# A pair of query products written with seven block products, in a hybrid decoder layer

## The chip, the cores and the metric

The kernel runs on one core of a Trainium2 chip. The metric is the device time of one execution in microseconds (us). TensorE (PE) multiplies matrices, VectorE (DVE) and ScalarE (ACT) work elementwise, GpSimd (POOL) does a few elementwise operations and issues transfers, SyncE (SP) issues the loads of weights. Products accumulate in PSUM, which has eight banks of 128 x 512 numbers; everything else lies in SBUF or in device memory.

## The reference

One decoder layer over 256 tokens of width 2048, in float32: a feed-forward (width 5632), a mixer (windowed attention beside a recurrent part, both gated), a cross-attention into a memory of 256 tokens, a second feed-forward, a final norm. The part at hand is the first of the mixer:

```python
def gated_parallel_mixer(x, norm_g, w_in, sinks, ...):
    h = rms_norm(x, norm_g)
    p = h @ w_in
    c = np.cumsum([ATTN_WIDTH, KV_WIDTH, KV_WIDTH, RWKV_COLS]).tolist()
    q, k, v, p_rwkv, gates = jnp.split(p, c, axis=-1)
    y_attn = sliding_window_attention(q, k, v, sinks)
...
```

The queries `q` are the first 1024 columns of `p`: 16 heads of 64.

## The kernel before

**Numbers in two parts.** A float32 operand is held as a high part `hi` (rounded to the format that PE takes) and a low part `lo`, the rest. A product of two such operands is three matmuls: hi hi, hi lo, lo hi (`times`, L470 to L475; one line for each). Weights come from device memory into `raw` buffers; ACT casts `hi` from them (L396), DVE subtracts to get `lo` (L397). The normed activations are held in features x tokens, in `xhi` and `xlo`, 16 chunks of 128 features by 256 tokens; `Norm.block` (L681) makes four chunks from 512 columns of x by transposes on PE (L661), a cast on ACT (L688) and a subtraction on DVE (L689). The factor of the norm for each token, `r`, is applied to the product.

**A plain product** (`product`, L451) computes 256 tokens x 512 columns. It runs over the 16 chunks in eight pairs (`KU` = 2); for each pair it does two token blocks `t` x two chunks x three matmuls of 128 x 128 by 128 x 512. Its two sums stand in two banks of the `acc` ring (three banks).

**A product of pairs** (`product_pair`, L533) computes 256 tokens x two blocks of 512 columns at once. For a pair of chunks this is a product of a 2 x 2 by a 2 x 2 block matrix: eight block products, or seven by a scheme of Strassen's kind. For the seven it needs sums of the weights (`divide`, L425 to L428, four on DVE for a pair, then divided into `thi` and `tlo` by `two_parts`) and sums of the activations (`combinations`, L485: a sum of hi and lo, L505; four sums of 128 x 128 numbers, L511 to L514; a cast, L521; a subtraction, L524). The seven go to sums called p1 to p7 in PSUM: p1, p3, p5 in the `mm` ring, p2, p4 and q in `acc`, p6, p7 in `tr`, so all eight banks are in use. `first`, `middle` and `out` put them together. Which pairs of chunks are done with seven is a tuple in the plan of weights. The first feed-forward does gate and up so for three of eight pairs (`SEVEN`), its down products for three of eight or two of six.

**Order of the work.** `weight_plan` (L101) lists all weights in the order of use; from it come `units` (a block of 256 rows x 512 columns, 512 KB) and `items` (one unit, or two for a pair). `next_item` (L432) asks for the loads of the coming units, divides the weights of this item, and divides ahead up to `AHEAD` = 2 units. Loads go to SP's queue in that order. In the mixer the `raw` ring has four buffers of one unit; `hi` and `lo` rings have three of one unit each. In the feed-forwards loads use four buffers of two units (L341).

Background work (`Interleave`) is a set of generators that advance by a step at each `bg.tick()` between groups of matmuls. The compiler's planner then gives buffers out and orders each engine's instructions by estimated times, with the program's order as priority, so the order on an engine can differ from the program's a little. `tc.issue_after(ins)` puts an instruction behind another on its engine.

**At the change.** The last down product of the first feed-forward adds to x (L634), its columns are written out (L819) and turned into chunks 8 to 15 of the mixer's activations. Then the mixer begins: memory of the first stage is reused by its own pool, most of it a ring `t4` of 23 tiles of 4 KB a partition; a tile is reused when the one that lay there is free. The two plain products of L873 follow, each with eight items of one unit: `scaled` (L844) copies the two sums to `tok` with the factor `r` on ACT (L847), and `to_features` transposes them to `qt` (L866, L867) in the background. Then comes the product for keys and values (L879), and the attention (`attend`) behind it. `STAGE_AT` (L42) holds numbers of items at which sums of weights for the second feed-forward are made ahead.

Of the kernel before, what the change touches and what calls it, by code (L numbers as in the profile page):

```python
# [7 lines left out]
F32 = mybir.dt.float32  # L8
# [30 lines left out]
SEVEN, SEVEN_DOWN = (0, 2, 4), ((2, 4, 6), (2, 4))  # L39
SEVEN_2, STAGED = (0, 2, 3, 4), (3,)  # L40

STAGE_AT = [266 + 2 * n for n in range(10)]  # L42


class Act:
# [55 lines left out]
def weight_plan(a):  # L101

    w = {n: v[0] for n, v in a.items() if "_w_" in n or n.startswith("w_")}
    yield from feed_forward_plan(w["ffn1_w_gate"], w["ffn1_w_up"], w["ffn1_w_down"], False)
    yield None
    w_in = w["w_in"]
    cols = [0, 512, ATTN_W]
    for c in cols:  # L110
        yield w_in, 0, KD, c, 512
    yield w_in, 0, KD, C_RW + 3 * RW, 288
    for h in range(2):
        yield w_in, 0, KD, C_RW + RW + h * 512, 512
    for n in range(4):
        yield w_in, 0, KD, C_GATE + n * 512, 512
        yield w["w_proj_attn"], 0, 8, n * 512, 512
    for h in range(2):
        yield w_in, 0, KD, C_RW + h * 512, 512
        yield w_in, 0, KD, C_RW + 2 * RW + h * 512, 512  # L120
    for n in range(4):
        yield w_in, 0, KD, C_GATE + D + n * 512, 512
    for n in range(4):
        yield w["w_proj_rwkv"], 0, 8, n * 512, 512
    for n in range(4):
        yield w["w_out"], 0, KD, n * 512, 512
    yield w["w_cross_kv"], 0, KD, 0, 512
    yield w["w_cross_q"], 0, KD, 0, 512
    yield w["w_cross_kv"], 0, KD, 512, 512
    for n in range(4):  # L130
        yield w["w_cross_o"], 0, 4, n * 512, 512
    yield None
    yield from feed_forward_plan(w["ffn2_w_gate"], w["ffn2_w_up"], w["ffn2_w_down"], True)
# [3 lines left out]
def decoder_layer(ctx: ExitStack, tc: tile.TileContext, a: dict, out: bass.AP):  # L137
# [171 lines left out]
    for entry in weight_plan(a):  # L309
        if entry is None:  # L310
            ends.append(len(units))
            continue
        plan.append(entry)
        w, k0, nk, c0, n = entry
        if not isinstance(w, tuple):
            for k in range(k0, k0 + nk, KU):
                items.append(((len(units),), False))
                units.append((w, k, c0, n))
            continue
        for k in range(k0, k0 + nk, 2 * KU):  # L320
            u = len(units)
            units += [(v, k + i, c, 512) for v, c in zip(w, c0) for i in (0, KU)]
            for i in range(2):
                q = (k - k0) // KU + i
                if n == SEVEN_2 and q in STAGED:
                    staged[len(items)] = len(staged)
                items.append(((u + i, u + 2 + i), q in n))
    raws, parts, summed = {}, {}, {}
    first_unused = {items[i][0][1] for i in staged}
    sums_d = dram.tile([len(staged), P, 4, 512], F32, name="sums")  # L330
    at = {"item": 0, "product": 0, "pool": None}

    def load(u, pieces=None):

# [64 lines left out]

    def two_parts(v, e):  # L400
        sp = at["pool"]
        hi = sp.tile([P, KU, 512], F32R, tag="thi" + e, name="thi")
        lo = sp.tile([P, KU, 512], F32R, tag="tlo" + e, name="tlo")
        act.copy(hi[:], v[:])  # L404
        dve.tensor_tensor(lo[:], v[:], f32(hi[:]), ALU.subtract)  # L405
        return hi, lo

    def divide(i):


        if i >= len(items) or i in parts:
            return
        which, seven = items[i]
        if len(which) == 1:
            parts[i] = split_unit(*which)
            return
        g, u = which
        if not seven:
            parts[i] = split_unit(g), split_unit(u)
            return  # L420
        t = summed.get(i)
        if t is None:
            rg, ru = raws[g], raws[u]
            t = [wp.tile([P, KU, 512], F32, tag="raw", name="raw", bufs=4) for _ in range(2)]
            dve.tensor_tensor(t[1][:, 0], ru[:, 0], rg[:, 0], ALU.subtract)  # L425
            dve.tensor_tensor(t[0][:, 0], ru[:, 1], ru[:, 0], ALU.subtract)
            dve.tensor_tensor(t[0][:, 1], ru[:, 1], t[1][:, 0], ALU.subtract)  # L427
            dve.tensor_tensor(t[1][:, 1], rg[:, 1], t[0][:, 1], ALU.subtract)  # L428
        a_ = two_parts(t[0], "a")
        parts[i] = split_unit(g), split_unit(u, slice(1, 2)), (a_, two_parts(t[1], "b"))  # L430
# [54 lines left out]
    def combinations(sp, x: Act, seven, name, ready=lambda: True, early=True, n=0):  # L485

        pairs = [q for q in range(max(seven) + 1) if early or q in seven]
        n = n or sum(4 if q in seven else 2 for q in pairs)  # L490
        parts = [sp.tile([P, n, P], F32R, tag=name + e, name=name + e) for e in ("hi", "lo")]
        c = {"parts": parts, "at": {}, "done": False, "seven": seven, "early": early}

        def work():
            o = 0
            while not ready():
                yield
            for q in pairs:
                while not {2 * q, 2 * q + 1} <= x.done:
                    yield  # L500
                t = wp.tile([P, KU, 512], F32, tag="raw", name="raw", bufs=4)
                v = t[:, 0].rearrange("p (k t n) -> p k t n", k=2, t=2)
                f = t[:, 1].rearrange("p (i n) -> p i n", i=4)
                with tc.issue_after(at["lo"].ins):
                    dve.tensor_tensor(  # L505
                        t[:, 0].rearrange("p (k n) -> p k n", k=2), f32(x.at(0, 2 * q, 2)),
                        f32(x.at(1, 2 * q, 2)), ALU.add,
                    )
                if q in seven:
                    n = 4  # L510
                    dve.tensor_tensor(f[:, 0], v[:, 0, 1], v[:, 1, 1], ALU.add)  # L511
                    dve.tensor_tensor(f[:, 1], f[:, 0], v[:, 0, 0], ALU.subtract)
                    dve.tensor_tensor(f[:, 2], v[:, 0, 0], v[:, 0, 1], ALU.subtract)
                    dve.tensor_tensor(f[:, 3], v[:, 1, 0], f[:, 1], ALU.subtract)  # L514
                else:
                    n = 2
                    dve.tensor_tensor(f[:, :2], v[:, :, 0], v[:, :, 1], ALU.subtract)
                yield
                s = slice(o, o + n)
                with tc.issue_after(at["hi"].ins):  # L520
                    act.copy(parts[0][:, s], f[:, :n])  # L521
                yield
                with tc.issue_after(at["lo"].ins):
                    dve.tensor_tensor(parts[1][:, s], f[:, :n], f32(parts[0][:, s]), ALU.subtract)  # L524
                c["at"][q] = o
                o += n
                yield
            c["done"] = True

        bg.spawn("mem", work())  # L530
        return c

    def product_pair(x: Act, c, w, first, middle, out):  # L533
# [20 lines left out]
            return [x.at(p, k)[:, t * P : (t + 1) * P] for p in range(2)]  # L554

        def of_c(q, i):
            return [p[:, c["at"][q] + i, :] for p in c["parts"]]

        def of_w(parts_, i):
            return [p[:, i, :] for p in parts_]  # L560
# [1 line left out]
        for q in range(nk // KU):  # L562
            k = KU * q
            if q in seven:
                bg.until(lambda: c["done"] and (q > min(seven) or not bg.groups["feat"][1]))
                g, u, s = next_item()
                end = q == max(seven)
                ta, tb = s
                for i, (to, x_, w_) in enumerate((
                    ("p7", of_c(q, 2), of_w(ta, 0)), ("p6", of_c(q, 1), of_w(ta, 1)),  # L570
                    ("p1", of_x(0, k), of_w(g, 0)), ("p2", of_x(0, k + 1), of_w(g, 1)),
                    ("p3", of_c(q, 3), of_w(u, 1)), ("p4", of_x(1, k + 1), of_w(tb, 1)),
                    ("p5", of_c(q, 0), of_w(tb, 0)),
                )):
                    add(to, x_, w_, end and to in ("p1", "p5", "p6", "p7"))
                    if i % 2:
                        bg.tick()
                    if end and to == "p1":
                        first(b)
                if end:  # L580
                    middle(b)
                continue
            g, u = next_item()
            early, last = q < max(seven), q == nk // KU - 1
# [243 lines left out]
    with tc.tile_pool(name="mx", bufs=1, reuse_waits="tile") as sp:  # L828
# [3 lines left out]
        def t4(name, shape=(P, 4, T), dt=F32):  # L832
            return sp.tile(list(shape), dt, tag="t4", name=name, bufs=N4)

        for i, n in staged.items():
            bg.spawn("stage", stage(t4, i, n))

# [6 lines left out]
        def scaled(pb, r, n=512):  # L844
            s = t4("tok", (P, 2, 512))
            for t in range(2):
                act.activation(s[:, t, :n], pb[t][:, :n], AF.Copy, scale=r[t])  # L847
            return s

        C4 = [0, P, 2 * P, 3 * P]  # L850
# [14 lines left out]
        def to_features(tok, dst, name):  # L865
# [2 lines left out]
                yield  # L868
            bg.seen.add(name)

        qt = []
        for h in range(2):
            tok = scaled(product(n2.x, W["w_in"]), n2.r)  # L873
            qt.append(t4("qt"))
            bg.spawn("feat", to_features(tok, qt[h], "q"))

        kd = t4("kd")
        vt = t4("vt", (P, 2, KV_W))
# [760 lines left out]
```

## Time and profile before

| | |
|---|---|
| median of 3 runs | 2247.78 us (2247.43 to 2248.47) |
| profiled execution | 2248.79 us, of which the profile's span is 2247.1 us |
| PE busy | 2231.4 us (99%) |
| DVE busy | 1820.5 us (81%) |
| ACT busy | 1245.0 us (55%) |
| bytes moved | 461.35 MB, mean 205 GB/s |
| the two query products | from 715.3 us to about 762 us of the span |

A row of the timeline has the start and the duration in us, the engine, the line in the kernel, the operation, the tile written and the tiles read, shapes, a count, and in brackets the idle time before it with what ended it. A row of a stage has the stretch and its length, the busy time and count of instructions of PE, PEld (PE's loading of weights), DVE, ACT and POOL, the granted PE clock, the busy share of the transfer engines and GB/s. A row of grouped instructions has total busy us, mean ns of one, and the idle time of the engine just before them, with what ended it. Matmuls overlap one another, so a PE that is busy all the time can still go from one matmul to the next faster than a duration says: starts are what counts.

### The profile page before, as it was taken

The numbers are of one execution on the slowest core, as the hardware profiler recorded it, in microseconds if no ns is written. First come the engines' busy times: TensorE is split into PE (matmuls) and PEld (weight loads), VectorE is DVE, ScalarE is ACT, GpSimd is POOL, SyncE is SP. The second block draws the span as 40 slices with busy tenths as digits, with TensorE's granted clock in tenths as the row PEclk, the third lists the DMA queues.
The fourth block names the chain that finished last, engine by engine and source line by source line (L and its number), as shares of the span: only waits on it lengthen the run. The fifth ranks groups of instructions, "written<-read, shape, count | busy, mean of one in ns | idle before, by whom it ended". The sixth has DMA issues, their size and how long they took to land.

```text
span 2247.1 us, 28239 instructions
## 1 busy us (share of the span) xinstructions
PE 2231.4 (99%) x10587; PEld 1833.6 (82%) x10587; DVE 1820.5 (81%) x2342; ACT 1245.0 (55%) x1621; POOL 134.9 (6%) x192
## 2 busy tenths in 40 slices
PE   9999999999999999999999999999999999999998
PEld 7888888888888877788888888888888888888886
DVE  7898988998989476977656666547999999999997
ACT  6555555555556567544444446456665466555654
POOL 1000000000001000201320040001000000000002
PEclk9999999999999999999999999999999999999999
DMA  7555555556556544676767576547565566556564
GB/s 264 187 201 197 201 198 202 200 188 212 195 193 201 169 135 150 198 231 207 224 214 263 187 258 227 190 167 272 197 237 204 195 231 218 201 205 221 197 229 146
DMA packets 229225, 461.35 MB, mean 205 GB/s; under 512 B 15227, under 2 KB 17504, under 8 KB 229088
## 3 DMA queue, kind: packets, MB, share of 16 engines
q1 hardware_dynamic: 220512, 433.62, 56.8%
q0 software_dynamic: 8112, 25.12, 3.5%
q8 instruction: 83, 1.36, 0.2%
q10 hardware_dynamic: 464, 0.79, 0.1%
q14 instruction: 54, 0.44, 0.1%
HBM read 435.91 MB, written 23.59 MB: 204 GB/s over the span
## 4 chain that ended last, share of the span: by engine, by line
PE 95%; DVE 2%; DMA 1%; issue 1%; ACT 1%; SPq 0%; POOL 0%; POOLq 0%; DVEq 0%; ACTq 0%
PE acc L473 19%; PE acc L474 19%; PE acc L475 19%; PE mm L475 8%; PE mm L474 8%; PE mm L473 8%; PE tr L661 2%; PE tr L474 2%; PE tr L473 2%; PE tr L475 2%; PE mm L1313 1%; DVE lo L397 1%; PE tr L1249 1%; DMA raw<-in_w_out_dram 0%; PE mm L903 0%
## 5 line engine op out<-in xcount | busy, mean ns | idle before, releaser
L396 ACT CAST hi<-raw 128x1024 fp32r<-128x1024 f32 (+1 forms) x770 | 756.5, 992 | 714.4 <-PE acc L475 514.8
L397 DVE TENSOR_TENSOR lo<-raw,hi 128x1024 fp32r<-128x1024 f32 (+1 forms) x770 | 886.1, 1153 | 315.5 <-ACT hi L396 314.0
L473 PE MATMUL acc<-hi,xhi 128*128 128x512 f32 (+1 forms) x1166 | 462.2, 397 | 2.1 <-ACT xhi L688 1.7
L474 PE MATMUL acc<-lo,xhi 128*128 128x512 f32 (+1 forms) x1166 | 452.7, 388 | 0.0
L475 PE MATMUL acc<-hi,xlo 128*128 128x512 f32 (+1 forms) x1166 | 452.5, 388 | 0.0
L473 PEld LDWEIGHTS acc<-hi,xhi 128*128 128x128 f32 x1166 | 219.4, 188 | 49.8 <-issue 4.0
L475 PEld LDWEIGHTS acc<-hi,xlo 128*128 128x128 f32 x1166 | 218.8, 188 | 46.0 <-DVE xlo L689 1.0
L474 PEld LDWEIGHTS acc<-lo,xhi 128*128 128x128 f32 x1166 | 219.2, 188 | 43.8 <-issue 1.7
L404 ACT CAST thi<-raw 128x1024 fp32r<-128x1024 f32 x192 | 199.9, 1052 | 62.9 <-DVE raw L427 42.4
L405 DVE TENSOR_TENSOR tlo<-raw,thi 128x1024 fp32r<-128x1024 f32 x192 | 232.2, 1219 | 1.1 <-ACT thi L404 0.4
L474 PE MATMUL acc<-lo,hhi 128*128 128x512 f32 x372 | 145.5, 391 | 0.8 <-DVE lo L397 0.8
L475 PE MATMUL acc<-hi,hlo 128*128 128x512 f32 x372 | 145.5, 391 | 0.0
L473 PE MATMUL mm<-hi,xhi 128*128 128x512 f32 x370 | 145.4, 393 | 0.0
L473 PE MATMUL acc<-hi,hhi 128*128 128x512 f32 x372 | 144.9, 390 | 0.0
L475 PE MATMUL mm<-hi,xlo 128*128 128x512 f32 x370 | 144.3, 390 | 0.0
L474 PE MATMUL mm<-lo,xhi 128*128 128x512 f32 x370 | 144.2, 390 | 0.0
L474 PEld LDWEIGHTS acc<-lo,hhi 128*128 128x128 f32 x372 | 69.9, 188 | 15.4 <-DVE lo L397 1.2
L473 PEld LDWEIGHTS acc<-hi,hhi 128*128 128x128 f32 x372 | 69.9, 188 | 14.3
L475 PEld LDWEIGHTS mm<-hi,xlo 128*128 128x128 f32 x370 | 69.4, 188 | 14.6
L475 PEld LDWEIGHTS acc<-hi,hlo 128*128 128x128 f32 x372 | 69.9, 188 | 14.0
L474 PEld LDWEIGHTS mm<-lo,xhi 128*128 128x128 f32 x370 | 69.5, 188 | 14.2
L473 PEld LDWEIGHTS mm<-hi,xhi 128*128 128x128 f32 x370 | 69.5, 188 | 14.0
(396 smaller groups left out, 3595.7 us busy)
## 6 DMA issues: line engine op xcount, KB each, us to landing
raw<-in_ffn_w_down_dram SPq DMA_DIRECT2D x88, 1024.0 KB, 5.1
raw<-in_ffn_w_gate_dram SPq DMA_DIRECT2D x84, 1024.0 KB, 5.1
raw<-in_ffn_w_up_dram SPq DMA_DIRECT2D x78, 1024.0 KB, 6.2
raw<-in_w_in_dram SPq DMA_DIRECT2D x136, 512.0 KB, 3.5
raw<-in_w_out_dram SPq DMA_DIRECT2D x32, 512.0 KB, 4.4
raw<-sums SPq DMA_DIRECT2D x20, 512.0 KB, 6.3
raw<-in_w_proj_attn_dram SPq DMA_DIRECT2D x16, 512.0 KB, 4.4
raw<-in_w_proj_rwkv_dram SPq DMA_DIRECT2D x16, 512.0 KB, 4.8
```

The costliest lines, as they stand in the source:

```text
L396: at["hi"] = act.copy(hi[:, s], raw[:, s])
L397: at["lo"] = dve.tensor_tensor(lo[:, s], raw[:, s], f32(hi[:, s]), ALU.subtract)
L404: act.copy(hi[:], v[:])
L405: dve.tensor_tensor(lo[:], v[:], f32(hi[:]), ALU.subtract)
L473: pe.matmul(o, xh, hi, start=first, stop=False, **how)
L474: pe.matmul(o, xh, lo, start=False, stop=False, **how)
L475: pe.matmul(o, xl, hi, start=False, stop=last, **how)
L661: pe.transpose(b[:, o : o + P], tok[:, t, col : col + P], ident[:])
L1249: pe.matmul(b[e][:, o : o + P], x1[r, j, cs_], x2[r, j, cs_], start=True, stop=True)
L1313: pe.matmul(vb[:, (o + k) * P : (o + k + 1) * P][:, r], lhs(k, e), rhs[:, k, r], start=first and k + e == 0, stop=True, **ek,)
```

## The change

The two blocks of 512 query columns become one entry of the plan, with pairs 2, 4 and 6 of the eight pairs of chunks done with seven products. Its units alternate between the two column blocks, and an entry is recognised in the loop over the plan by `len(ends) == 1` (between the two feed-forwards). There are eight items of two units where there were sixteen of one; `STAGE_AT` moves by eight.

`room` is new: outside of the feed-forwards, sums and their parts are kept in the mixer's `t4` ring instead of `raw` buffers or tiles of their own. `combinations` can be called without a pool and then keeps a tile of hi and lo parts for each pair. `scaled_pair` is new: it calls `product_pair` with its own `first`, `middle` and `out`. The flag `at["sevens"]` is set and read nowhere.

```diff
+SEVEN_Q = (2, 4, 6)
+
-STAGE_AT = [266 + 2 * n for n in range(10)]
+STAGE_AT = [258 + 2 * n for n in range(10)]
...
-    cols = [0, 512, ATTN_W]
-    for c in cols:
-        yield w_in, 0, KD, c, 512
+    yield (w_in, w_in), 0, KD, (0, 512), SEVEN_Q
+    yield w_in, 0, KD, ATTN_W, 512
...
+        if len(ends) == 1:
+            for q in range(nk // KU):
+                items.append(((len(units), len(units) + 1), q in n))
+                units += [(v, k0 + KU * q, c, 512) for v, c in zip(w, c0)]
+            continue
...
+    def room(name, dt=F32):
+
+        if at["pool"] is None:
+            return at["t4"](name, (P, KU, 512), dt)
+        return wp.tile([P, KU, 512], F32, tag="raw", name="raw", bufs=4)
...
     def two_parts(v, e):
         sp = at["pool"]
-        hi = sp.tile([P, KU, 512], F32R, tag="thi" + e, name="thi")
-        lo = sp.tile([P, KU, 512], F32R, tag="tlo" + e, name="tlo")
+        if sp is None:
+            hi, lo = room("thi", F32R), room("tlo", F32R)
+        else:
+            hi = sp.tile([P, KU, 512], F32R, tag="thi" + e, name="thi")
+            lo = sp.tile([P, KU, 512], F32R, tag="tlo" + e, name="tlo")
...
-            t = [wp.tile([P, KU, 512], F32, tag="raw", name="raw", bufs=4) for _ in range(2)]
+            t = [room("sums") for _ in range(2)]
...
-                t = wp.tile([P, KU, 512], F32, tag="raw", name="raw", bufs=4)
+                t = room("sums")
...
-                s = slice(o, o + n)
+                if parts:
+                    hi, lo = (p[:, o : o + n, :] for p in parts)
+                else:
+                    p = room(name, F32R)[:].rearrange("p a (b n) -> p (a b) n", n=P)
+                    hi, lo = p[:, :n], p[:, 4 : 4 + n]
...
+        def scaled_pair(c, w):
+
+            s = [t4("tok", (P, 2, 512)) for _ in range(2)]
+            u = t4("u", (P, 2, 512))
+            u2, u3 = u[:, 0], u[:, 1]
+
+            def first(b):
+                act.copy(s[0][:, 0], b["p1"][:])
+                act.copy(s[1][:, 1], b["q"][:])
+
+            def middle(b):
+                dve.tensor_tensor(u2, b["p6"][:], s[0][:, 0], ALU.add)
+                dve.tensor_tensor(u3, b["p7"][:], u2, ALU.add)
+                dve.tensor_tensor(u2, b["p5"][:], u2, ALU.add)
+                dve.tensor_tensor(s[1][:, 1], s[1][:, 1], u3, ALU.add)
+
+            def out(b, to):
+                t, n = int(to in ("p4", "p5")), int(to in ("p3", "p5"))
+                o = s[n][:, t]
+                more = {"p2": o, "p4": u3, "p3": u2, "p5": o}[to]
+                dve.tensor_tensor(o, b[to][:], more, ALU.add)
+                act.activation(o, o, AF.Copy, scale=n2.r[t])
+
+            product_pair(n2.x, c, w, first, middle, out)
+            return s
...
+        cx = combinations(None, n2.x, SEVEN_Q, "c", early=False)
         qt = []
-        for h in range(2):
-            tok = scaled(product(n2.x, W["w_in"]), n2.r)
+        for tok in scaled_pair(cx, W["w_in"]):
             qt.append(t4("qt"))
-            bg.spawn("feat", to_features(tok, qt[h], "q"))
+            bg.spawn("feat", to_features(tok, qt[-1], "q"))
```

More of the change, by code (lines that the diff above doesn't have):

```diff
@@ L330, in decoder_layer @@
     sums_d = dram.tile([len(staged), P, 4, 512], F32, name="sums")
-    at = {"item": 0, "product": 0, "pool": None}
+    at = {"item": 0, "product": 0, "pool": None, "sevens": False}
+    def room(name, dt=F32):
+        if at["pool"] is None:
+            return at["t4"](name, (P, KU, 512), dt)
+        return wp.tile([P, KU, 512], F32, tag="raw", name="raw", bufs=4)
     def load(u, pieces=None):
@@ L490, in combinations @@
         n = n or sum(4 if q in seven else 2 for q in pairs)
-        parts = [sp.tile([P, n, P], F32R, tag=name + e, name=name + e) for e in ("hi", "lo")]
-        c = {"parts": parts, "at": {}, "done": False, "seven": seven, "early": early}
+        parts = sp and [
+            sp.tile([P, n, P], F32R, tag=name + e, name=name + e) for e in ("hi", "lo")
+        ]
+        c = {"at": {}, "done": False, "seven": seven, "early": early}
         def work():
@@ L518, in work @@
                 yield
-                s = slice(o, o + n)
+                if parts:
[3 more added lines that the diff above has]
+                    hi, lo = p[:, :n], p[:, 4 : 4 + n]
                 with tc.issue_after(at["hi"].ins):
-                    act.copy(parts[0][:, s], f[:, :n])
+                    act.copy(hi, f[:, :n])
                 yield
                 with tc.issue_after(at["lo"].ins):
-                    dve.tensor_tensor(parts[1][:, s], f[:, :n], f32(parts[0][:, s]), ALU.subtract)
-                c["at"][q] = o
+                    dve.tensor_tensor(lo, f[:, :n], f32(hi), ALU.subtract)
+                c["at"][q] = hi, lo
                 o += n
@@ L556, in of_c @@
         def of_c(q, i):
-            return [p[:, c["at"][q] + i, :] for p in c["parts"]]
+            return [p[:, i, :] for p in c["at"][q]]
         def of_w(parts_, i):
@@ L565, in product_pair @@
                 bg.until(lambda: c["done"] and (q > min(seven) or not bg.groups["feat"][1]))
+                at["sevens"] = True
                 g, u, s = next_item()
@@ L581, in product_pair @@
                     middle(b)
+                    at["sevens"] = False
                 continue
@@ L833, in t4 @@
             return sp.tile(list(shape), dt, tag="t4", name=name, bufs=N4)
+        at["t4"] = t4
         for i, n in staged.items():
```

## The prediction

> **What bounds the kernel now.** I read the page's busy shares and its chain of waits first, then busy times by stage, then the timeline around the two products that change.
>
> ```profile
> span 2247.1 us, 28239 instructions
> PE 2231.4 (99%) x10587; PEld 1833.6 (82%) x10587; DVE 1820.5 (81%) x2342; ACT 1245.0 (55%) x1621; POOL 134.9 (6%) x192
> PE 95%; DVE 2%; DMA 1%; issue 1%; ACT 1%; SPq 0%; POOL 0%; POOLq 0%; DVEq 0%; ACTq 0%
> 600.00:660.00 60.00, 60.00 (x274) 49.46 (x273) 53.39 (x71) 33.77 (x40) 0.00 (x0) 1.00 0.61 210
> 660.00:702.00 42.00, 42.00 (x193) 34.19 (x192) 41.28 (x55) 26.15 (x39) 1.51 (x2) 1.00 0.59 201
> 715.30:762.00 46.70, 46.70 (x219) 38.77 (x218) 25.91 (x31) 25.84 (x40) 6.60 (x25) 1.00 0.64 203
> 715.30:728.20 12.90, 12.90 (x66) 10.79 (x65) 11.26 (x19) 9.69 (x20) 3.54 (x7) 1.00 0.74 238
> ```
>
> TensorE (PE) is the bound: 95% of the chain, busy without a gap in all these stretches, granted clock 1.00. So a matmul less is worth its spacing, if its operands are ready. The stage rows give PE, weight load, VectorE (DVE), ScalarE (ACT), GpSimd, clock, DMA. 715.3 to 762 are the two query products; DVE is busy 25.9 of 46.7 us there, but 11.3 of 12.9 in the first part. In the feed-forward before (660 to 702), where products of seven already run, DVE is busy 41.3 of 42 and PE still never idles: DVE may be nearly full, not more.
>
> **What is removed.**
>
> ```profile
> 715.28 0.39 PE L473 MATMUL acc<-hi,xhi 128*128 128x512 f32 x1
> 715.96 0.39 PE L473 MATMUL acc<-hi,xhi 128*128 128x512 f32 x1
> 737.74 0.69 ACT L847 ACTIVATE tok<-acc,rs 128x512 f32<-128x512 f32 x1 [0.30 <-PE acc L475]
> 739.10 0.69 ACT L847 ACTIVATE tok<-acc,rs 128x512 f32<-128x512 f32 x1 [0.67 <-PE acc L475]
> 761.82 0.69 ACT L847 ACTIVATE tok<-acc,rs 128x512 f32<-128x512 f32 x1 [0.67 <-PE acc L475]
> L661 PE MATMUL tr<-ident,x 128*128 128x128 f32 x16 | 2.2, 272 | 0.0
> ```
>
> Three matmuls start within 715.96 - 715.28 = 0.68 us: 0.227 each (the 0.39 of a row overlaps the next). A pair of chunks costs eight products of three matmuls, 24 x 0.227 = 5.44 us; with seven, 21 x 0.227 = 4.76. Three pairs of eight: 9 matmuls, **2.04 us less**. That is all that PE can win; 0.2% of this kernel, what a measurement tells from no change, is 4.5 us. The 16 transposes of the last blocks of x stay: the first product ends near 739.0, 23.7 us after its start, of which 96 x 0.227 = 21.8 is its own, so they take 1.9.
>
> **What is added, on DVE.** The same kind of work stands in the trace at the start of the first down product, with all its prices:
>
> ```profile
> 190.07 0.69 DVE L505 TENSOR_TENSOR raw<-hhi,hlo 128x512 f32<-128x512 f32 x1
> 190.68 0.68 DVE L667 TENSOR_TENSOR hlo<-tr,hhi 128x512 fp32r<-128x512 f32 x1
> 191.28 0.28 DVE L511 TENSOR_TENSOR raw<-raw 128x128 f32<-128x128 f32 x1
> 191.48 0.29 DVE L513 TENSOR_TENSOR raw<-raw 128x128 f32<-128x128 f32 x1
> 193.28 0.69 DVE L427 TENSOR_TENSOR raw<-raw,raw 128x512 f32<-128x512 f32 x1
> 193.89 0.69 DVE L524 TENSOR_TENSOR dlo<-raw,dhi 128x512 fp32r<-128x512 f32 x1
> 194.49 0.69 DVE L428 TENSOR_TENSOR raw<-raw,raw 128x512 f32<-128x512 f32 x1
> 195.09 1.23 DVE L397 TENSOR_TENSOR lo<-raw,hi 128x1024 fp32r<-128x1024 f32 x1
> 196.23 1.23 DVE L405 TENSOR_TENSOR tlo<-raw,thi 128x1024 fp32r<-128x1024 f32 x1
> 197.36 0.69 DVE L397 TENSOR_TENSOR lo<-raw,hi 128x512 fp32r<-128x512 f32 x1
> ```
>
> By the spacing of starts, 128x512 takes 0.60, 128x1024 1.13, 128x128 0.20. A plain pair divides two blocks of weights: 2.26. A seven pair makes four sums (2.4), two low parts of the sums (2.26), one whole and one half low part (1.73): 6.39. The combinations of the left side cost 0.60 + 4 x 0.20 + 0.60 = 2.0 a pair, 6.0 for three. The ends are four additions in `middle` and four in `out`, 4.8.
>
> Now the due times. DVE, in the order that the program gives, from 715.7:
>
> ```profile
> 714.58 1.22 DVE L397 TENSOR_TENSOR lo<-raw,hi 128x1024 fp32r<-128x1024 f32 x1
> 715.71 1.28 DVE L634 SCALAR_TENSOR_TENSOR x<-acc,x 128x512 f32<-128x512 f32 x2
> 718.59 0.88 DVE L689 SCALAR_TENSOR_TENSOR xlo<-tr,gains,xhi 128x256 fp32r<-128x256 f32 x2 [0.41 <-ACT xhi L688]
> 726.07 0.16 DVE L707 TENSOR_REDUCE ms<-ss 128x2 f32<-128x8 f32 x1
> ```
>
> Four last additions into x (2.4) and the eight low parts of x (8 x 0.40 = 3.2), the norm's 0.35, pair 1 (2.26), the combinations of pair 2 (2.0), pair 2's sums and first low part (3.53): 13.7, that is 729.4; if the first step of pair 4's combinations (1.4) goes ahead, 730.8. PE reaches pair 2 at 715.28 + 10.9 + 1.9 = 728.1. Up to the start of pair 6 the same sum is 2.4 + 3.2 + 0.35 + three plain pairs 6.8 + two sevens 12.8 + combinations 6.0 + 3.53 = 35.1, so 750.8; PE comes at 715.28 + 21.8 + 9.5 + 1.9 = 748.5. **DVE is 2.3 us late**: for this stretch it becomes the bound.
>
> Some of that is absorbed, as the down product shows:
>
> ```profile
> 196.22 0.62 PE L473 MATMUL tr<-thi,dhi 128*128 128x512 f32 x2
> 196.68 0.39 PE L473 MATMUL mm<-hi,hhi 128*128 128x512 f32 x1
> 197.50 0.50 PE L474 MATMUL tr<-tlo,dhi 128*128 128x512 f32 x1
> ```
>
> PE came at pair 2 at 196.22, the low part `tlo` was done at 196.23 + 1.23 = 197.46, and PE filled the time with matmuls that need it not; about 1.1 us of lateness is covered so. Left: 2.3 - 1.1 = 1.2 us.
>
> **Weight loads.** The change moves no load to another queue: 16 of 512 KB on SP as before, now in the order of the pairs, and the sums go to the mixer's ring without any transfer. But the raw ring has four buffers, two pairs: pair 6 is asked for when pair 4's blocks are divided.
>
> ```profile
> raw<-in_w_in_dram SPq DMA_DIRECT2D x23, 512.0 KB, 3.5
> DMA to landing us min/median/max: 3.3/4.4/4.8
> L397 DVE TENSOR_TENSOR lo<-raw,hi 128x1024 fp32r<-128x1024 f32 x17 | 20.7, 1223 | 19.6 <-ACT hi L396 19.6
> ```
>
> A load takes 3.5 (median, 690 to 790), 4.4 where two follow at once (700 to 740). After pair 4's last block DVE has 1.13 + 2.26 = 3.4 to do: 1.0 us exposed at pair 6; pair 4's own load lies behind the rest of the combinations. Bounds: 0 (the hi ring holds DVE back anyway) and 4.4 - 2.26 = 2.1 for each of pairs 4 and 6. I take 1.0. Waits of DVE on ACT's casts in this order (0.41 in a row above): from 0 to 1, taken 0.3.
>
> **Rest.**
>
> ```profile
> L404 ACT CAST thi<-raw 128x1024 fp32r<-128x1024 f32 x192 | 199.9, 1052 | 62.9 <-DVE raw L427 42.4
> ```
>
> ACT casts 3.5 blocks for a seven pair in place of two, 1.5 x 1.05 = 1.6 us more, 4.7 for three, gains the copies in `first` and keeps its four scalings; it was busy 25.8 of 46.7 (0). The 4.8 of DVE at the end lie beside pair 7 (5.44 us) and the key product, where DVE waits 19.6 us in 17 pieces now; without that cover the key product would start up to 2.4 later. All eight PSUM banks are in use until pair 6 ends; the transposes of the queries come after, so nothing waits for them but the attention, behind the key product. The stage's items shift by eight with the eight items fewer (0); the flag `sevens` is read nowhere (0).
>
> **Sum.** -2.04 + 1.2 + 1.0 + 0.3 = +0.5 us. The profiled span 2247.1 becomes 2247.6, its execution 2248.79 (1.7 outside the span) becomes 2249.3; the median of the runs is 1.0 below that execution: **2248.3**.
>
> **Rivals.** *B, all hidden*: the planner fills PE with other matmuls as at 196, the late 2.3 us vanish: -2.04, 2245.7. For it: PE idles nowhere in 660 to 702. Against: there DVE had one pair's combinations left to do, here three, and x besides. *C, the raw ring*: the loads of pairs 4 and 6 come 2.1 late each, and PE then has no matmul at hand to fill with, so the 1.1 is lost too: 2.3 + 4.2 + 0.3 - 2.04 = +4.8, 2252.6, slower. It passes 4.5 us from 3.9 us of late loads. For it: four buffers of one block here, where the first stage has four of two blocks (L341). Against: of the hi ring's three buffers a pair takes two, so DVE waits for PE before it divides the second block of the next pair, and a pair's loads have that time too.
>
> *D, memory of x*: the mixer's ring lies over the first stage's tiles, and the combinations may get buffers in x's place, free only when its last readers are done.
>
> ```profile
> 718.49 0.71 POOL L819 DMA_DIRECT2D x1d<-x  x1 [0.48 <-DVE x L634]
> 726.09 0.31 POOL L198 MEMSET abias<- 128x256 f32 x1 [6.89 <-ACT junk L697]
> DMA to landing us min/median/max: 3.3/5.4/14.2
> ```
>
> The constant `abias` waits so until 726.1. Ahead of them DVE has 2.4 + 3.2 + 0.35 + 2.26 = 8.2 us of work, to 723.9, then idles 2.2: +0.5 + 2.2 = +2.7, 2250.5. If the copy of x landed as late as the slowest here, 718.49 + 14.2 = 732.7, it is +9.3; over 4.5 from a release at 727.9. The copy's median puts it before 726.1, so I take 2250.5.
> The Trainium skill, "TensorE: Matmul & The Clock Gate", section "Architectural detail: the array is 16× 32×32, not 1× 128×128", says that ACT and DVE take their queues strictly in turn, which speaks for D: one combination that waits holds all weights behind it. By it the whole idle time counts; if DVE could pass it by, D would come out at the forecast. The row at 718.59, where DVE idles 0.41 for a cast, agrees and doesn't prove it.
> The same page, section "HAM oscillation — how this bites in real kernels", has PE's clock halve after gaps of over about 3.4 us: an estimate from its window of 3.4 us is 1.7 us more on D's upper end. No run here shows it; all granted clocks above are 1.00.
>
> **Chances.** Forecast 0.45 (2246.5 to 2250), B 0.22, C 0.15, D 0.14, of it 0.04 above 727.9; 0.04 for a changed order further on, half of it faster. Slower by over 4.5 us: 0.15 + 0.04 = 0.19; faster by as much: 0.02; within: 0.79. The range takes in B with its 0.4 below, D and C: 2245.3 to 2253.2.
>
> **What would show it.** Right: PE's count falls by 9; PE idles in 2 to 3 us in all between 728 and 752, at pairs 2 and 6, released by `tlo`, the combinations' low part or `lo`; DVE busy over 90% there; the rows from the key product on are shifted as a whole. C: DVE idles for DMA raw before the sums of pairs 4 and 6. D: DVE idles for ACT junk or the copy of x before 728. B: no idle PE. The prediction is wrong if PE idles over 5 us there, or if the stretches after 762 change their length by more than 1 us.

## The result and the profile after

The changed kernel takes **2257.94 us** (median of 4 runs, 2257.2 to 2258.45) beside 2247.7 for the kernel before, measured with it (4 runs, 2247.43 to 2248.47): ratio 1.0044, 95% interval 1.0032 to 1.0057. It is 10.2 us slower. The forecast was 2248.3 with a range up to 2253.2; both missed. The profiled execution took 2258.04 us with a span of 2256.3, so the median may be read from it within 0.1.

The page first: span and instructions, and busy time by engine.

```profile
span 2256.3 us, 28278 instructions
PE 2233.6 (99%) x10578; PEld 1832.4 (81%) x10578; DVE 1844.3 (82%) x2386; ACT 1251.6 (55%) x1632; POOL 134.7 (6%) x192
```

Nine matmuls fewer, as reckoned (10587 to 10578), and yet PE is busy 2.2 us longer (2231.4 to 2233.6): some of them ran slower. DVE has 23.8 us more of work. The averages show nothing else; the stage rows do. Columns: stretch, length, busy time (and count) of PE, PEld, DVE, ACT and GpSimd, granted PE clock, share and GB/s of the transfers; of the kernel after:

```profile
715.30:762.00 46.70, 39.98 (x165) 30.05 (x163) 38.95 (x63) 25.98 (x41) 7.51 (x25) 0.93 0.47 152
728.00:730.00 2.00, 1.48 (x7) 0.91 (x5) 1.97 (x5) 0.00 (x0) 2.00 (x5) 1.00 0.00 0
730.00:732.00 2.00, 0.00 (x0) 0.00 (x0) 0.08 (x1) 0.85 (x3) 1.91 (x12) 1.00 0.00 0
732.00:734.00 2.00, 1.31 (x3) 0.48 (x3) 0.85 (x3) 2.00 (x3) 0.20 (x4) 0.92 0.00 0
734.00:736.00 2.00, 1.65 (x3) 0.83 (x3) 2.00 (x7) 0.18 (x2) 0.00 (x0) 0.50 0.00 0
736.00:738.00 2.00, 1.02 (x2) 0.83 (x3) 2.00 (x3) 1.31 (x2) 0.00 (x0) 0.50 0.45 118
738.00:740.00 2.00, 2.00 (x6) 1.61 (x5) 2.00 (x3) 1.17 (x2) 0.00 (x0) 0.50 0.89 298
740.00:742.00 2.00, 2.00 (x9) 1.56 (x9) 1.90 (x3) 1.06 (x2) 0.00 (x0) 0.87 1.01 338
746.00:762.00 16.00, 13.82 (x57) 9.93 (x55) 14.10 (x18) 9.52 (x11) 0.00 (x0) 1.00 0.47 149
```

Where PE was full for 46.7 us it is now busy 39.98. Pair 1 ends near 728, where the forecast had it (728.1), and six matmuls of pair 2 that need no sums run on to 729.5. From 730 PE, DVE and the transfers stand still, and up to 731.15 only GpSimd works. Later PE's clock is at half for some 6.8 us (by the rows, 0.08 x 2 / 0.5 = 0.3 before 734, 6 up to 740, and 0.13 x 2 / 0.5 = 0.5 after). Smaller holes of 16.00 - 13.82 = 2.2 us together lie between 746 and 762, at pairs 4 and 6.

From its first matmul to the first of the key product the query stretch takes 54.9 us (715.2 to 770.2), and 45.4 in the kernel before without eight transposes that fell into it: 9.5 more, with 2.04 of matmuls fewer, so 11.5 were lost. They have three parts. PE idles 46.70 - 39.98 = 6.7. Eleven matmuls between 734 and 740 ran at a spacing of about 0.43 in place of 0.227 (rows below), 0.2 more each: 2.2. The other 2.6 or so is a remainder. It fits matmuls that came singly, with starts 0.34 to 0.6 apart, but it is not split further here.

Who holds whom is read from the timeline (start, duration, engine, line, tiles, idle time before and its releaser), again of the kernel after, chosen rows of all engines in order of time:

```profile
725.87 0.60 ACT L408 CAST hi<-raw 128x512 fp32r<-128x512 f32 x1
726.03 0.31 POOL L199 MEMSET abias<- 128x256 f32 x1 [6.89 <-ACT junk L720]
...
729.10 0.39 PE L490 MATMUL acc<-hi,xlo 128*128 128x512 f32 x1
731.15 0.30 ACT L231 CAST ones_r<-bdones 128x128 fp32r<-128x128 f32 x1 [4.67 <-POOL bdones L222]
731.35 0.29 ACT L231 CAST ones_r<-bdmean 128x128 fp32r<-128x128 f32 x1
731.55 1.04 ACT L408 CAST hi<-raw 128x1024 fp32r<-128x1024 f32 x1
732.50 0.62 ACT L542 CAST c<-sums 128x512 fp32r<-128x512 f32 x1
732.65 0.51 PE L488 MATMUL acc<-hi,xhi 128*128 128x512 f32 x1 [3.16 <-ACT hi L408]
733.15 0.69 DVE L545 TENSOR_TENSOR c<-sums,c 128x512 fp32r<-128x512 f32 x1 [3.06 <-ACT c L542]
735.88 1.05 ACT L419 CAST thi<-sums 128x1024 fp32r<-128x1024 f32 x1 [1.82 <-DVE sums L442]
736.98 1.22 PE L488 MATMUL tr<-thi,c 128*128 128x512 f32 x2 [1.22 <-ACT thi L419]
738.00 0.63 PE L489 MATMUL acc<-lo,xhi 128*128 128x512 f32 x1
738.43 0.63 PE L490 MATMUL acc<-hi,xlo 128*128 128x512 f32 x1
```

Read it backwards from 732.65. PE has waited 3.16 for the high part of pair 2's weights. That cast stood on ACT behind two casts of `ones_r`, constants of the mixer that PE reads for the first time at 1109. They stood still 4.67 for GpSimd, which makes the mixer's constants one after another, and GpSimd could start only at 726.03, released by ACT's last pass over x (`junk`). At 733.15 DVE, too, has idled 3.06: the combinations' cast was behind the same two. So ACT's queue held up both PE and DVE. The kernel before has the same two casts 0.9 us earlier, and PE waited for nothing in that stretch. A whole block of weights had been cast ahead of them there, in the change half a block:

```profile
725.94 1.03 ACT L396 CAST hi<-raw 128x1024 fp32r<-128x1024 f32 x1
...
730.29 0.30 ACT L230 CAST ones_r<-bdones 128x128 fp32r<-128x128 f32 x1 [3.32 <-POOL bdones L221]
```

Behind the queries the kernel is the old one. The stretch from 762 of before answers to that from 770 of after; first before, then after, each with one write-out of the second feed-forward's input far behind:

```profile
762.00:842.00 80.00, 78.72 (x438) 61.24 (x437) 51.95 (x119) 48.62 (x119) 2.99 (x6) 1.00 0.45 135
```

```profile
770.00:850.00 80.00, 78.50 (x440) 60.84 (x439) 52.80 (x120) 49.65 (x114) 2.98 (x6) 1.00 0.45 138
```

```profile
1521.26 0.77 POOL L1552 DMA_DIRECT2D x3d<-x  x1 [73.92 <-DVE x L1551]
```

```profile
1531.06 0.76 POOL L1602 DMA_DIRECT2D x3d<-x  x1 [73.92 <-DVE x L1601]
```

9.8 us of shift at 1521, and 9.2 between the two spans: the loss is made in the query stretch.

### The profile page after: what moved, and what is told of

Same layout as the page of the kernel before. It is cut to its first block, busy times and chain, and to the rows that moved or that the text cites. A ratio compares the mean times of both kernels' runs of the same rounds, so it can differ in the third digit from the quotient of the medians.

```text
span 2256.3 us, 28278 instructions
## 1 busy us (share of the span) xinstructions
PE 2233.6 (99%) x10578; PEld 1832.4 (81%) x10578; DVE 1844.3 (82%) x2386; ACT 1251.6 (55%) x1632; POOL 134.7 (6%) x192
## 4 chain that ended last, share of the span: by engine, by line
PE 94%; DVE 2%; issue 1%; DMA 1%; ACT 1%; POOL 0%; SPq 0%; POOLq 0%; DVEq 0%; ACTq 0%
PE acc L488 19%; PE acc L489 19%; PE acc L490 19%; PE mm L489 8%; PE mm L490 8%; PE mm L488 8%; PE tr L684 2%; PE tr L489 2%; PE tr L488 2%; PE tr L490 2%; PE mm L1363 1%; PE tr L1299 1%; DVE lo L409 1%; DMA raw<-in_w_out_dram 0%; PE mm L953 0%
## 5 line engine op out<-in xcount | busy, mean ns | idle before, releaser
L488 PE MATMUL acc<-hi,xhi 128*128 128x512 f32 (+1 forms) x1133 | 450.1, 398 | 5.5 <-ACT hi L408 3.2
L490 PE MATMUL acc<-hi,xlo 128*128 128x512 f32 (+1 forms) x1133 | 440.4, 389 | 0.0
L489 PE MATMUL acc<-lo,xhi 128*128 128x512 f32 (+1 forms) x1133 | 440.3, 389 | 0.0
L488 PEld LDWEIGHTS acc<-hi,xhi 128*128 128x128 f32 x1133 | 213.4, 188 | 53.0 <-ACT hi L408 4.2
L490 PEld LDWEIGHTS acc<-hi,xlo 128*128 128x128 f32 x1133 | 212.9, 188 | 44.9 <-DVE xlo L712 1.0
L489 PEld LDWEIGHTS acc<-lo,xhi 128*128 128x128 f32 x1133 | 213.3, 188 | 42.6 <-issue 1.7
L488 PE MATMUL mm<-hi,xhi 128*128 128x512 f32 x385 | 151.6, 394 | 0.3 <-ACT hi L408 0.3
L490 PE MATMUL mm<-hi,xlo 128*128 128x512 f32 x385 | 150.1, 390 | 0.0
L489 PE MATMUL mm<-lo,xhi 128*128 128x512 f32 x385 | 150.1, 390 | 0.0
```

The lines of the kernel that those rows point to most:

```text
L488: pe.matmul(o, xh, hi, start=first, stop=False, **how)
L489: pe.matmul(o, xh, lo, start=False, stop=False, **how)
L490: pe.matmul(o, xl, hi, start=False, stop=last, **how)
```

## The experiments

Three things were to be told apart: ACT's queue held by the constants, DVE's load ahead of the pairs of seven, and the clock; beside them the forecast's own terms, the raw ring and the memory of x. Times are differences of the medians to the kernel before in the same set of runs; the runs of one kernel there lie 1 to 5.5 us apart, so the ratio's interval decides.

**1. The two casts late.** They go behind the scalings of the key product on ACT; the rest of the changed kernel keeps its order.

```diff
-            act.copy(r[:], v[:])
+        def casts(ins):
+            for r, v in zip(ones_r, (bdones, bdmean)):
+                with tc.issue_after(ins):
+                    act.copy(r[:], v[:])
...
+        casts(scaling.ins)
```

> The changed kernel, with the two casts of the constant matrices of ones (ones_r) put behind the key product's scalings on ACT instead of in front of pair 2's casts; all other instructions in the same order. Theory: ACT stood 4.7 us at these casts, which wait for GpSimd's constants, and the casts of pair 2's weights and combinations stood behind them. Without it PE's wait of 3.2 us before pair 2 falls to under 1.5 and the granted clock stays at 1.00 through 728 to 744: 3.2 + 3.4 us of the 10.2 come back, 2251 (2250 to 2252.5). Rival: DVE's backlog makes pair 2 as late by itself; the wait stays at 3 us or more, now for DVE (the combinations' low part or tlo), the clock falls again, and the time stays at 2255 or more.

2254.41 us, +5.6, ratio 1.0026 (1.0017 to 1.0035): 4.6 of the 10.2 come back, and 5.6 don't; the time lies between what the two theories expected. The first hole is gone, another stands in its place. Stage rows, then timeline rows, of this kernel:

```profile
730.00:732.00 2.00, 1.41 (x5) 0.49 (x4) 2.00 (x6) 0.60 (x1) 1.91 (x12) 1.00 0.00 0
732.00:734.00 2.00, 0.00 (x0) 0.00 (x0) 2.00 (x3) 0.96 (x1) 0.32 (x4) 1.00 0.00 0
734.00:736.00 2.00, 1.86 (x4) 1.49 (x5) 2.00 (x4) 1.13 (x2) 0.00 (x0) 0.50 0.93 258
736.00:738.00 2.00, 2.00 (x7) 1.61 (x6) 2.00 (x2) 1.15 (x2) 0.00 (x0) 0.64 0.86 259
```

```profile
732.28 0.68 DVE L447 TENSOR_TENSOR sums<-raw,sums 128x512 f32<-128x512 f32 x1
733.04 1.04 ACT L424 CAST thi<-sums 128x1024 fp32r<-128x1024 f32 x1 [2.43 <-DVE sums L447]
734.13 1.22 PE L493 MATMUL tr<-thi,c 128*128 128x512 f32 x2 [2.51 <-ACT thi L424]
734.62 1.21 DVE L425 TENSOR_TENSOR tlo<-sums,thi 128x1024 fp32r<-128x1024 f32 x1
```

DVE is now busy 2.00 of 2 from 730 to 738 while PE waits: it is DVE that is late here, and ACT's cast only passes the wait on. The two causes stand one behind the other, and each theory was half right.

**2. The same two casts late in the kernel before** (a control, the same edit).

> Control: the kernel before with the same two casts moved. ACT stood 3.3 us there too, but nothing was late behind it. Theory and rival both: 2247.7, no change within 0.5 us; if it is faster by over 1 us, the casts cost something in the kernel before as well and the comparison of the first run has to be corrected by it.

2249.32 us, +0.5, ratio 1.0003 (0.9994 to 1.0012): no change. So the place of the casts costs nothing here, where nothing that is due stands behind them.

**3. PE kept at work in the hole.** Fourteen matmuls of 128 x 128 that nobody reads are put between pairs 1 and 2, into a free bank; in the trace they take PE from 728.00 to 731.04.

```diff
+                if at["pool"] is None and q == min(seven):
+                    warm = tr()
+                    with tc.issue_after(at["mm"].ins):
+                        for _ in range(14):
+                            pe.matmul(warm[:, :P], ones[:], ones[:], start=True, stop=True)
```

> The changed kernel with 14 matmuls of 128x128 ones into a free bank between pair 1 and pair 2, about 3.2 us of PE work that nobody reads, in the place of the idle time. Theory: the drop of the granted clock to 0.50 (732 to 741) is a cost of its own behind the wait; with the fillers the clock stays 1.00 and 1.5 to 3.4 us come back: 2254.5 to 2256.5. Rival: DVE is the bound behind the gap (busy 2.00 of 2 us in each slice from 734 to 744), the slow matmuls cost nothing, and the time stays within 0.7 us of 2257.9.

2256.99 us, +8.2, ratio 1.0036 (1.0023 to 1.005): some 2 us less than the change. The clock stays at 1.00 up to 736, then falls all the same, as the next hole, a wait of 1.95 us for a low part on DVE, is still there (stage rows of this kernel):

```profile
734.00:736.00 2.00, 1.11 (x4) 0.59 (x4) 2.00 (x7) 0.18 (x2) 0.00 (x0) 1.00 0.00 0
736.00:738.00 2.00, 0.94 (x2) 0.83 (x3) 2.00 (x3) 1.31 (x2) 0.00 (x0) 0.76 0.45 60
```

The 2 us fit half of the slow time taken away, but the two intervals overlap, and the clock's own price isn't isolated by it. That it is a consequence of the holes, and not their cause, the row of 734 to 736 does show: there PE idles at full clock.

**4. The raw ring.** The first kernel with the query weights loaded into the mixer's ring, up to six units ahead.

```diff
+        elif "t4" in at and u < ends[0] + 16:
+            raw = at["t4"]("rawq", (P, KU, n))
```

> As the first run, and the query product's weights are loaded into the t4 ring, up to six units ahead in place of four. Theory of the raw ring: DVE's wait of 1.9 us for a load ahead of pair 6 and ACT's of 0.8 and 0.7 go, 1 to 1.5 us faster than the first run. Rival: the hi ring holds DVE back anyway, within 0.5 us of the first run.

2254.03 us, +5.2, ratio 1.0024 (1.0014 to 1.0033), against 1.0026 of the first: no gain that can be told. The wait of DVE for a load (0.8 in the first kernel) is gone and PE waits for ACT's high parts in its place (1.4 and 1.3 us). The loads were late, and nothing that could be told hung on it.

**5. The combinations in their turn.** The first kernel, with the combinations of pairs 4 and 6 begun only when the pair of seven before them is under way, so that pair 2's weights pass them on DVE.

```diff
-                while not {2 * q, 2 * q + 1} <= x.done:
+                while not {2 * q, 2 * q + 1} <= x.done or (not sp and q > 2 and at["item"] < base + q - 1):
...
-                bg.until(lambda: c["done"] and (q > min(seven) or not bg.groups["feat"][1]))
+                bg.until(lambda: (c["done"] or at["pool"] is None and q in c["at"]) and (q > min(seven) or not bg.groups["feat"][1]))
```

> As the first run (casts late), and the combinations of pairs 4 and 6 are begun only when pairs 2 and 4 are under way, so DVE makes pair 2's sums first. Theory: what is left of the wait before pair 2 (2.5 us for thi) is DVE's backlog; 1.4 us of it were pair 4's combinations, so the wait falls to about 1.0, the clock drops less or not at all, and 2 to 3.5 us come back against the first run: +2 to +3.5 over the kernel before. Rival: the wait is that of ACT's casts and the weights' loads, and the order of DVE's small sums changes it by less than 0.5 us: +5 to +5.6.

2251.02 us, +1.8, ratio 1.0009 (1.0001 to 1.0018): another 3.8 us back. The whole stretch and the waits of PE (for what, total, times, longest) of this kernel:

```profile
715.30:762.00 46.70, 44.51 (x196) 34.51 (x195) 45.08 (x70) 28.83 (x43) 8.26 (x25) 1.00 0.60 192
```

```profile
PE acc L493 <- ACT hi L413: 1.0, 2, 0.7
PE tr L493 <- ACT thi L424: 0.8, 1, 0.8
PE mm L493 <- ACT hi L413: 0.3, 1, 0.3
```

```profile
730.55 0.68 DVE L447 TENSOR_TENSOR sums<-raw,sums 128x512 f32<-128x512 f32 x1
```

The sum that pair 2's `thi` waits for starts at 730.55 instead of 732.28 (1.7 earlier), the wait for it falls from 2.51 to 0.8, and with that the clock stays at 1.00. So 1.7 us of order on DVE were worth 3.8 on PE, by the medians. What remains of PE's waits, 2.1 us, is for ACT's high parts; DVE is busy 45.08 of 46.7, and which of the two holds the other is not shown.

**6. Two pairs of seven.** The first kernel with `SEVEN_Q = (4, 6)`; pair 2 is plain again.

> Casts late, and only pairs 4 and 6 done with seven (six matmuls fewer than the kernel before, 1.36 us). Theory: the first seven falls after DVE's rush at the stage's start, so PE meets no wait before pair 4 and the clock stays 1.00; -1.4 to +0.5 us against the kernel before. Rival: the pairs as such (items of two units, four raw buffers, three hi buffers) are late wherever the sevens stand: +3 us or more.

2249.65 us, +0.4, ratio 1.0005 (0.9996 to 1.0014). The loss is gone, and no gain is seen. PE's only wait of the stretch, and DVE's wait for a load ahead of pair 6:

```profile
PE tr L494 <- DVE tlo L425: 0.6, 2, 0.3
```

```profile
744.26 0.69 DVE L445 TENSOR_TENSOR sums<-raw 128x512 f32<-128x512 f32 x1 [1.98 <-DMA raw<-in_w_in_dram]
```

A load that DVE waited 1.98 for cost PE at most the 0.6: DVE was some five us ahead of PE, which began that pair's sums at 749.57.

**7. Two pairs of seven, casts where the change had them** (`SEVEN_Q = (4, 6)` alone).

> Pairs 4 and 6 with seven, the casts of ones where the change had them. Theory of the casts: pair 2 is now a plain pair, and its casts still stand behind those of ones, so PE waits about 3 us before pair 2 as in the changed kernel and the clock drops; 4 to 6 us more than the run with the casts late. Rival: the casts matter only together with the sums of a seven; within 1 us of the run with the casts late.

2251.14 us, +1.9, ratio 1.0009 (1.0 to 1.0018). A miss: 4 to 6 us above kernel 6 were expected, 1.5 came, and the two intervals overlap. ACT stood still 4.23 for the constants here as well, but a whole block of pair 2's weights had been cast ahead of them, so PE did not stop at pair 2; the delay came out at pairs 4 and 6, as 1.9 us of waits for `tlo` (0.6 in kernel 6) and 0.5 for `thi`. The casts are harmful by what stands behind them, not by their own 4 us.

**8. Pairs without any seven.** The first kernel with all eight pairs plain (192 matmuls), still as one entry of two column blocks.

> Casts late, all eight pairs plain: the query blocks in pairs of units, four sums in four banks, the same 192 matmuls as the kernel before. Theory: without sums and combinations DVE is never late; within 0.7 us of the kernel before. Rival: the form in pairs costs by itself: +2 us or more.

2248.52 us, -0.7, ratio 0.9998 (0.9989 to 1.0007), no wait of PE. Joining the two blocks into one product costs nothing that can be told.

**9. Two pairs of seven, casts late, combinations in turn.**

> Seven products at pairs 4 and 6 only, the casts of the constants behind the key product's scalings, and the combinations of pair 6 begun only when pair 4 is under way. If VectorE's load ahead of the first pair of seven is what is left of the loss (the theory), no wait of PE of over 1 us in the query stretch, clock 1.00, and the time is 0.3 to 1.4 us below the kernel before (six matmuls of 0.227 us removed, 1.4 us, less the waits). If the two pairs of seven cost something in themselves that the order does not touch (the rival), it stays where the two pairs with casts late stood: +0.4 us, within the measurement of no change.

2247.33 us, -1.4, ratio 0.9996 (0.9987 to 1.0005). PE waits for nothing in the query stretch:

```profile
715.30:762.00 46.70, 46.70 (x213) 38.15 (x213) 42.12 (x63) 28.98 (x43) 8.93 (x25) 1.00 0.68 204
```

The median lies where six matmuls fewer would put it (6 x 0.227 = 1.4), and the interval holds no change: it beats the changed kernel, and that it beats the kernel before isn't shown.

**10. The combinations off x's memory.** The first kernel with an unused tile of 9 KB a partition ahead of the `t4` ring, which shrinks from 23 tiles to 21 to make room.

> The kernel with the casts late, and a pad ahead of the combinations' ring so that none of it lies over the queries' memory. If what is left of the loss there is VectorE's and ScalarE's load before pair 2 (the theory), it is the same as without the pad: +5 to +6 us against before, and PE waits some 2.5 us for ScalarE's cast of a high part. If VectorE stands still for the queries' memory (the forecast's rival of the memory of x), 2 to 4 us come back: +1.5 to +3.5 us.

2261.58 us, +12.8, ratio 1.0061 (1.0045 to 1.0076): neither expected it. The query stretch is that of kernel 1 (here first kernel 10, then 1), the loss is made by 1200, in the recurrent part:

```profile
715.30:762.00 46.70, 42.80 (x182) 32.77 (x181) 42.93 (x67) 28.43 (x42) 7.58 (x25) 0.96 0.54 170
1100.00:1200.00 100.00, 97.27 (x656) 81.73 (x654) 56.82 (x76) 39.96 (x63) 28.79 (x47) 1.00 0.69 217
```

```profile
715.30:762.00 46.70, 42.76 (x182) 32.93 (x181) 43.19 (x68) 28.37 (x42) 7.71 (x25) 0.96 0.55 172
1100.00:1200.00 100.00, 99.42 (x702) 86.37 (x701) 62.91 (x85) 43.24 (x68) 29.05 (x46) 1.00 0.74 236
```

So DVE didn't stand still for x's memory, as the rival said it would. That the two tiles fewer in the mixer's ring delay the recurrent part is likely, and not tested. The total is no evidence on the queries; the stretch is.

**11. Combinations in turn alone,** the casts where the change had them: the fourth field.

> The changed kernel with the combinations of pairs 4 and 6 in their turn, and the two casts of constants left where the change had them, ahead of pair 2's weights on ScalarE. It fills the fourth field beside the change (+10.2), casts late (+5.6) and both (+1.8). If the two causes stand one behind the other (the theory), ScalarE's stop for GpSimd's constants is still there, a wait of PE of some 3 us for the high part of pair 2, and the time is +5 to +7 us, with the clock below 1.00 behind it. If VectorE's load was all of it and the casts only showed through it (the rival), it is +1.5 to +3 us.

2254.24 us, +5.2, ratio 1.0026 (1.0016 to 1.0036). PE's waits in this kernel:

```profile
PE acc L488 <- ACT hi L408: 3.9, 2, 3.2
PE mm L488 <- ACT hi L408: 0.3, 1, 0.3
```

The stop for the constants is there, the wait for `thi` is not. The four fields:

| against before, us | combinations ahead, as in the change | in turn |
|---|---|---|
| casts before pair 2's weights | +10.2 | +5.2 |
| casts late | +5.6 | +1.8 |

Taking away one cause is worth 4.6 or 3.4, the other 5.0 or 3.8; both together 8.4. They add nearly, so both are shown. The fields come from four sets of runs, the last on another chip than the first kernel's, each against the kernel before of its own set; the intervals of neighbours in the table overlap by 0.0004 of the time at most. Of the last 1.8, taking pair 2 out of the sevens gives all or nearly all back (+0.4 and -1.4, kernels 6 and 9).

## Why the prediction was wrong, point by point

**That PE is the bound, and the price of a matmul: right.** Nine fewer, and the two-pair kernel without waits (9) stands at the 1.4 us that six are worth, as far as its interval can tell. PE being the bound said only what could be won. The work added on DVE was right too: 3 x (6.39 - 2.26) + 6.0 + 4.8 = 23.2 us by the forecast's prices, 23.8 measured. What failed was when it was done.

**The step that failed first: "ACT casts 3.5 blocks for a seven pair in place of two ... it was busy 25.8 of 46.7 (0)", and "Waits of DVE on ACT's casts in this order ...: from 0 to 1, taken 0.3".** ACT's load was indeed covered: 25.98 of 46.70 after. Its *order* was not. The casts of the constants stood in ACT's queue and idled 3.32 us for GpSimd in the kernel before; the forecast quoted GpSimd's own late start at 726.1, and did not go on to who waits for GpSimd. In place of 0.3 the runs show 4.6 us for these two casts (kernel 1; 3.4 between kernels 11 and 5), with DVE waiting 3.06 for one cast and PE 3.16 for another. The instructions added on ACT were counted, those that they came to stand behind were not.

**The second: the due times on DVE, "729.4; if the first step of pair 4's combinations (1.4) goes ahead, 730.8".** With ACT's stop out of the way (kernel 1) the low part counted there is ready at 734.62 + 1.21 = 735.8, five us later. The sum had let the combinations begin at 723.9, as soon as DVE had the time; they stand behind the first stage's last step on DVE, and begin at 726.12, though the row at 726.07 that marks that step was quoted: 2.2. The other 2.8 went ahead of the low part as well: half a block's low part (0.6), a whole one of pair 2 (1.14), a step of the norm, and small sums that came 0.3 apart instead of 0.2. In the order of kernel 5 the same low part is ready at 733.15 + 1.21 = 734.4. The forecast's own figures had DVE 1.3 to 2.7 late at pair 2 (729.4 or 730.8 against 728.1), but it looked for the lateness at pair 6 and took 2.3 for it; it was at pair 2, where DVE has nothing in hand, and far larger. At pairs 4 and 6 PE idled 2.2 us between 746 and 762, near the 2.5 that the forecast had for that place (1.2, 1.0 and 0.3), but it is the smaller part, and little of it was the load: without the waits for loads (kernel 4) PE idles 0.9 at those two pairs, with them (kernel 1) 1.2.

**The clock: priced at nothing.** The forecast had holes of 2 to 3 us in all, and named the clock only beside the upper end of rival D. At 11 x 0.2 = 2.2 us it is a fifth of the loss, by the rows; no run isolates it.

**The raw ring, 1.0 at pair 6: seen, and its price not told from nothing.** DVE does wait for the load there, in the kernel after:

```profile
756.14 0.69 DVE L440 TENSOR_TENSOR sums<-raw 128x512 f32<-128x512 f32 x1 [1.87 <-DMA raw<-in_w_in_dram]
```

The wait is near the forecast's upper bound (2.1); taking it away gained nothing that can be told (kernel 4), and one of 1.98 cost at most 0.6 where PE had work in hand (kernel 6). So rival C, which ended nearest on the slower side at 2252.6, was not the cause either.

**Rival D, the memory of x: the right root, the wrong branch.** What D's row showed, GpSimd held until 726.03 by the last pass over x, cost nearly half of the loss, through ACT's queue; whether it is x's memory that holds GpSimd was not tried. That DVE idles for it (2.2, which brought D to +2.7) is excluded by kernel 10's stretch, and by the changed kernel itself: between 715 and 765 DVE waits there for casts of ACT and one load, and never for the last pass or the copy of x. **Rival B** needs PE to find other matmuls: it found six at 728 to 729.5 and ran out. **The ends and the rest of the kernel: right.** The stretch behind the queries has its old length within 0.2 us of PE's busy time, and the attention was not late by more than the shift. (The 19.6 us of waits that the forecast gave to the key product are a row of the query products, 715 to 762. From 762 to the key product's start PE is busy all the time.) The forecast's own mark for being wrong, PE idle for over 5 us between 728 and 752, was met: 24.00 less 18.62 busy, 5.4, and another 1.3 up to 762.

## What to carry to other kernels

When instructions move on an engine, list what already stands in that engine's queue around their new place and what each of these waits for; a stall that is harmless because nothing due stands behind it becomes the bound as soon as something does. A busy share of half (25.8 of 46.7) says nothing of a queue taken in order. When a scheme trades matmuls for sums, put its first use where the engine that makes the sums has had time to run ahead: here, with the constants out of the way, the same form lost 5.6 us with three uses from the third of eight pairs on, close behind another stage's end, and nothing that could be told with two from the fifth on; with three in a better order 1.8 were left.

## What the hardware showed that I had not expected

PE's granted clock fell to 0.50 behind holes that were shorter than I had thought necessary: a wait of 3.16 us in the change, of 2.51 in kernel 1 (with few matmuls in the 2 us before it), of 1.95 in kernel 3. It was back near 740 in the change, some 6.8 us later, and near 737 in kernel 1, some 3 later. In kernel 5, where the longest single wait was 0.8, it stayed at 1.00 throughout.

The length of one hole doesn't decide it. In kernel 4 two waits of 0.95 and 1.28 us, with one matmul between them, were enough; in kernel 7 two of 0.50 and 1.30, likewise with one matmul between them, were not. First kernel 4 (its longer wait, and the clock after it), then the whole stretch of kernel 7, with its clock at 1.00:

```profile
732.08 0.50 PE L498 MATMUL acc<-hi,xhi 128*128 128x512 f32 x1 [1.28 <-ACT hi L415]
734.00:736.00 2.00, 2.00 (x6) 1.43 (x5) 2.00 (x3) 1.76 (x3) 0.00 (x0) 0.50 0.64 150
```

```profile
715.30:762.00 46.70, 44.23 (x200) 35.45 (x199) 40.65 (x61) 27.94 (x44) 7.51 (x25) 1.00 0.66 192
```

The idle time together is 2.2 us in the one and 1.8 in the other. Each is a single profiled execution, and what tells them apart is not shown.

The Trainium skill, "TensorE: Matmul & The Clock Gate", section "HAM oscillation — how this bites in real kernels", has the clock fall behind idle gaps of over some 3.4 us. The halving agrees with the rows; the bound does not, with 1.28 to 3.16 measured here, and the measurement decides.
